# The sum of a bank's two halves one step behind ScalarE's copy, and modulation sums at most one per half tile

## The chip, the cores and the metric

The kernel runs on one core of a Trainium2 chip. A core has TensorE (PE, matrix products into PSUM), VectorE (DVE), ScalarE (ACT), GpSimd (POOL) and SyncE (SP, which issues most DMAs). Each engine works through its own queue in order and waits for the others by semaphores. The metric is the device time of one execution in microseconds (us); less is better.

## The reference

One decoder layer on 256 tokens of width 2048, in float32. A vector `c` gives six modulation rows; the part that this study is about is the token mixer.

```python
mod = silu(c) @ w_ada + b_ada            # 6 rows of 2048: shift, scale, gate, twice
h = rms_norm(x, norm1_g) * (1 + scale1) + shift1
proj = h @ w_in                          # (256, 2048) @ (2048, 9248)
lru_x = causal_conv(proj[lru x columns])
lru_out = gelu(proj[lru gate columns]) * rg_lru(lru_x, ...)
ssd_out = mamba2_heads(proj[z], proj[x, B, C], proj[dt], ...)
x = x + gate1 * (concat(lru_out, ssd_out) @ w_out)
h2 = rms_norm(x, norm2_g) * (1 + scale2) + shift2
x = x + gate2 * peer(h2, ...)            # top-16 experts of 16384 for 8 heads
out = rms_norm(x, final_norm_g)
```

In `mamba2_heads` the z columns go through `silu`; in the LRU part the gate columns go through `gelu`. These two kinds of columns are those whose evacuation is changed.

## The kernel before

**Exact products from rounded operands.** Weights come from memory in pieces of 128x1024 (`raw`). ScalarE copies a piece to a rounded high half `hl[:, 0]` (line 144), VectorE subtracts it from the raw piece and gets the low half `hl[:, 1]` (line 153, called "low half" below). The activations `hT` (tile `H`) are kept as a high and a low half too. A product is the sum of high x high, high x low and low x high. There are four buffers for `raw` and four for `hl`. In each half tile `issue_split` issues the high half of the piece four half tiles ahead, which has to wait until TensorE has left its buffer, then the low half of the piece before that one, three half tiles ahead; behind the low half the DMA of a new `raw` goes into SP's queue.

**Tiles.** The input projection makes 73 column tiles of 128 columns by 256 tokens, in the order of `ETILES`: first the SSD tiles with the SSD steps of four groups between them, then the LRU tiles. The first twelve go through `w_pass`, the other 61 (slots 0 to 60) through a loop of two half tiles each (`for h in range(2)`, lines 782 to 810), in PSUM bank `slot % 3`. Tiles of x, B, C, and LRU x are 256 columns wide in PSUM and take three matmuls per block (lines 796 to 798). Tiles of z (`32 <= e < 48`) and of the LRU gate (`e < 16`) take two, one of 512 columns that has high x high in the left half and high x low in the right half of the bank, and one of 256 (lines 449 and 451, `wide`). For those, the two halves of the bank have to be added. Of these 512-wide tiles the loop makes 26: 13 of z and 13 of the LRU gate.

**Order of the side work.** The program is written in the order in which each engine takes it. `defer(f, d)` puts `f` into a list that is run d half tiles after the next call of `mid()`; `mid()` runs once per half tile, behind `issue_split`. At the end of each tile its evacuation (`evac`) is deferred, so it runs in the first half of the next tile. What an evacuation defers in its turn runs in the second half. `bg_pop` takes one step of the SSD and LRU work per tile: its TensorE part at once, the rest deferred. The names that matter below:

- `halves(o, ps)`, lines 453 to 455: ScalarE copies the bank's right half to `o`, VectorE adds the left half to it; `o` is `ggt` (LRU gate) or the z tile (`X`, `zs`).
- `silu2`, lines 431 to 439: tanh on ScalarE into `stmp`, the product on VectorE one step later.
- `conv`, lines 421 to 429: ScalarE's first tap, three taps on VectorE one step later (line 426).
- `ada_step`, lines 378 to 407: one modulation step, a 128x1024 multiply-add on VectorE (line 389; line 386 for the first of sixteen), and the DMA of a new `adr` piece (two buffers). After sixteen, `fin` has 8 small matmuls (line 398) into the bank of the tile before (into bank 6 from slot 44).
- `ada_tick(rate, slot)`, lines 410 to 414: adds the rate (0.65 per SSD tile, 1.1 per LRU tile, 0.74 in the output projection) to a credit and runs a step for each whole credit.
- `lru_gates`: the matmuls of line 651, which read the conv's result `xct`; `lru_scan`: line 671 to 685; SSD: `Dm` (line 569), then the matmuls of lines 577 to 579.

Of the kernel before, what the change touches and what calls it, by code (L numbers as in the profile page):

```python
# [14 lines left out]
AF = mybir.ActivationFunctionType  # L15
OP = mybir.AluOpType
# [14 lines left out]
ADA_SSD, ADA_LRU, ADA_OUT = 0.65, 1.1, 0.74  # L31
# [27 lines left out]
def hybrid_kernel(ctx, tc, xT, cols, w_ada, w_in, lru_w, w_o1, w_o2, w_q, keys, u_t, v_t, fng, out):  # L59
    nc = tc.nc  # L60
    pe, act, dve, pool, sp = nc.tensor, nc.scalar, nc.vector, nc.gpsimd, nc.sync
# [9 lines left out]
    def bank(n):  # L71
        return psum.tile([128, 512], FT, name=f"b{n}")
# [3 lines left out]
    def xbuf(i):  # L76
        return pair[:, 4 * i:4 * i + 4] if i < 2 else keep.tile([128, 4, 256], FT, name=f"X{i}")
# [8 lines left out]
    def col(name, i=0, n=1):  # L86
        o, w = COLS[name]
        return cc[:, o + i:o + i + n]
# [78 lines left out]
    def defer(f, d=0):  # L167
        stages[d].append(f)
# [209 lines left out]
    def ada_step(slot):  # L378
        u = ada["use"]
        if u >= len(adq):  # L380
            return
        s, h, k = adq[u]
        w = adr.pop(u)
        if k == 0:
            ada["acc"] = mix.tile([128, 1024], FT, name="adacc", bufs=2)
            dve.tensor_scalar(ada["acc"], w, cact[:, 0:1], None, op0=OP.mult)
        else:
            a = ada["acc"]
            dve.scalar_tensor_tensor(a, w, cact[:, k:k + 1], a, op0=OP.mult, op1=OP.add)  # L389
        ada["use"] += 1  # L390
        ada_dma()
        if k == 15:
            a = ada["acc"]

            def fin():
                p = bank(ada["bank"])
                for i in range(8):
                    pe.matmul(p[:, i:i + 1], a[:, i * 128:(i + 1) * 128], ones[:, 0:1], start=True, stop=True)

                def add():  # L400
                    m = mod[:, s, 8 * h:8 * h + 8]
                    dve.tensor_add(m, p[:, :8], col("b_ada", 16 * s + 8 * h, 8))
                    if s == 3:
                        dve.scalar_tensor_tensor(m, m, 1.0, col("g2", 8 * h, 8), op0=OP.add, op1=OP.mult)
                defer(add)
            pedue.append((slot + 2, fin))

    adt = [0.0]

    def ada_tick(rate, slot):  # L410
        adt[0] += rate
        while adt[0] >= 1.0:
            adt[0] -= 1.0
            ada_step(slot)

# [5 lines left out]
    def conv(o, ps, w, bcol, after=None):  # L421
        act.activation(o, ps, AF.Identity, scale=w[3], bias=bcol)

        def taps():
            for d in (1, 2, 3):
                dve.scalar_tensor_tensor(o[:, d:], ps[:, :T - d], w[3 - d], o[:, d:], op0=OP.mult, op1=OP.add)
            if after:
                defer(after)
        defer(taps)

    def silu2(o, u, x, scale, on_pool):
        S["nt"] = (S["nt"] + 1) % 2
        t = S["tmp"][:, 2 + S["nt"]]
        act.activation(t, u, AF.Tanh, scale=scale)

        def pool_fin():
            pool.tensor_tensor(t, t, x, op=OP.mult)
            pool.tensor_tensor(o, t, x, op=OP.add)
        defer(pool_fin if on_pool else lambda: dve.scalar_tensor_tensor(o, t, 1.0, x, op0=OP.add, op1=OP.mult))
# [13 lines left out]
    def halves(o, ps):  # L453
        act.activation(o, ps[:, 256:], AF.Copy)
        dve.tensor_tensor(o, ps[:, :256], o, op=OP.add)

    S = {}
    acd = ctx.enter_context(tc.tile_pool(name="acd", bufs=1, space=bass.MemoryType.DRAM)).tile(
# [181 lines left out]
    LR = {"w": {}, "gg": {}}  # L640

    def lru_gates(b, i):
        h = 4 * b + i
        xc = LR["xc"][:, i]
        Z = {}

        def g_pe():
            w = LR["w"].pop(h)
            Z["p"] = p = bank(4 - (i + GD) % 2)
            for s in range(2):  # L650
                pe.matmul(p[:, s * 256:(s + 1) * 256], w[:, s], xc, start=True, stop=True)
            lru_w_load()

        def g_ew():
            if i == 0:
                LR.update(a=xbuf(0),
                          m=xbuf(1),
                          gx=keep.tile([128, 4, 256], FT, name="X2"))
            r, gx, p = LR["a"][:, i], LR["gx"][:, i], Z["p"]
            act.activation(r, p[:, :256], AF.Sigmoid, bias=col("lba", h))  # L660
            act.activation(gx, p[:, 256:], AF.Sigmoid, bias=col("lbi", h))
            act.activation(LR["m"][:, i], r, AF.Tanh, scale=lsp[:, h:h + 1])
            pool.tensor_tensor(gx, gx, xc, op=OP.mult)
        return g_pe, g_ew, 0
# [54 lines left out]
    def evac(e, ps):  # L719
        nonlocal y_ssd  # L720
        if e == 72:
            y_ssd = mix.tile([128, 16, 2, 256], FR, name="yssd", tag="Y1")
            S["BCs"] = mix.tile([128, 2, 2, 256], FT, name="BCs", tag=L[6])
            S["tmp"] = mix.tile([128, 4, 256], FT, name="stmp", tag=L[7])
            S["nt"] = 0
            dt_evac(ps)
        elif e >= 48:
            after = None
            if e >= 64:
                g = e % 4  # L730
                if e < 68:
                    S["BC"] = S["BCs"][:, g % 2]
                    for n, t in enumerate(("xs", "zs")):
                        S[t] = (mix.tile([128, 4, 256], FT, name=t) if g == 3 else
                                xbuf(2 * (g % 2) + n))
                o = S["BC"][:, (e - 64) // 4]
            else:
                i = e % 4
                g = (e - 48) // 4
                o = S["xs"][:, i]  # L740
                if i == 3:
                    ssd_steps(g)
            conv(o, ps, [hcw[:, (e - 48) * 4 + i:(e - 48) * 4 + i + 1] for i in range(4)],
                 hcb[:, e - 48:e - 47], lambda: silu2(o, o, o, 1.0, g == 0 or e < 64))
        elif e >= 32:
            i = e % 4
            o = S["zs"][:, i]
            if ps.shape[1] == 512:
                halves(o, ps)
                defer(lambda: silu2(o, o, o, 0.5, False))  # L750
            else:
                silu2(o, ps, ps, 0.5, False)
        elif e >= 16:
            b, i = divmod(e - 16, 4)
            if i == 0:
                LR["xc"] = mix.tile([128, 4, 256], FT, name="xct", tag="aa", bufs=3)
            conv(LR["xc"][:, i], ps, [col("lcw", (e - 16) * 4 + i_) for i_ in range(4)], col("lcb", e - 16))
            bg2.extend([(None, None, 0)] * (GD * (e == 16)) + [lru_gates(b, i)])
            if i == 3:
                bg2.extend(lru_scan(b) + lru_out(b))  # L760
        else:
            b, i = divmod(e, 4)
            if i == 0:
                LR["gg"][b] = mix.tile([128, 4, 256], FT, name="ggt", tag=(L[3], L[7], L[6], "aa")[b],
                                    bufs=3 if b == 3 else 1)
            if ps.shape[1] == 512:
                halves(LR["gg"][b][:, i], ps)
            else:
                act.activation(LR["gg"][b][:, i], ps, AF.Copy)

# [10 lines left out]
    slot = 0  # L781
    for e in ETILES[N0:]:
        ps = bank(slot % 3)
        two = e < 16 or 32 <= e < 48
        if not two:
            ps = ps[:, :256]
        for h in range(2):
            w = take()
            for kk in range(8):
                k = 8 * h + kk  # L790
                wh = w[:, 0, kk * 128:(kk + 1) * 128]
                wl = w[:, 1, kk * 128:(kk + 1) * 128]
                if two:
                    wide(ps, w, kk, hT, k)
                    continue
                pe.matmul(ps, wh, hT[:, k, 0, :], start=(k == 0), stop=False)  # L796
                pe.matmul(ps, wh, hT[:, k, 1, :], start=False, stop=False)  # L797
                pe.matmul(ps, wl, hT[:, k, 0, :], start=False, stop=(k == 15))  # L798
            issue_split()
            mid()  # L800
            if h == 0 and slot > 0:
                ada_tick(ADA_SSD if e >= 32 else ADA_LRU, slot)
        if e == 62:
            for _ in range(2):
                lru_w_load()
        bg_pop()
        ada["bank"] = 6 if slot >= 44 else (slot + 2) % 3
        pe_due(slot)
        defer(lambda e=e, ps=ps: evac(e, ps))
        slot += 1  # L810
# [54 lines left out]
    for n, k in enumerate(korder):  # L865
        w = take()
        y = y_ssd[:, k - 16] if k >= 16 else y_lru[k // 2][:, k % 2]
        for d in range(8):
            o = ob[d // 2][:, (d % 2) * 256:(d % 2) * 256 + 256]
# [38 lines left out]
    for d in range(8, 16):  # L908
        ps = bank(3 + d % 2)
# [735 lines left out]
```

## Time and profile before

| | us |
|---|---|
| median of 3 runs | 2152.05 |
| lowest and highest | 2142.25, 2161.91 |
| the profiled execution | 2157.51 |
| its span, first to last instruction | 2155.8 |
| idle of TensorE from 160 to 560 us | 14.3 |
| busy time of VectorE there | 328.8 of 400 |

The profile is one execution. A row names the line, engine and operation, the tiles written and read ("out<-in"), and for idle time the engine that ended it. [...] Where an instruction waits for several engines, the profile names the one that came last by its own reckoning, which need not be the right one. The stretch from 160 to 560 us holds the loop over the tiles. Its granted clock is given as a share of TensorE's full clock.

### The profile page before, as it was taken

The page shows a single profiled execution, that of the slowest core. Times are in us where ns is not written, and L with a number is a line of the kernel's source. Part 1 is how long each engine was busy: PE and PEld are TensorE (multiplying, and loading weights), DVE is VectorE, ACT ScalarE, POOL GpSimd, SP SyncE. Part 2 cuts the span into 40 slices and gives each one's busy share as a digit, 9 for nine tenths or more (in the row PEclk, how much of TensorE's full clock was granted, in tenths as well). Part 3 has the DMA queues.
Part 4 walks back from the last instruction along what each step waited for, and adds up shares of the span by engine and source line. Part 5 has one row for each costly group of instructions (what it writes and reads, how often), then busy time and mean ns, then how long its engine had stood idle before and what let it go on. Part 6 is the DMA issues. An engine that isn't in the chain of part 4 may idle for free.

```text
span 2155.8 us, 34802 instructions
## 1 busy us (share of the span) xinstructions
PE 2085.5 (97%) x13060; PEld 1633.2 (76%) x13060; DVE 1397.8 (65%) x2009; ACT 964.9 (45%) x1472; POOL 887.8 (41%) x728
## 2 busy tenths in 40 slices
PE   7999999999999999999999999999999999999996
PEld 4789989988999898888788778666666656555653
DVE  3378887977888869779889986433334353343434
ACT  3356656666644454444445444333333333333332
POOL 0013133412112110002325641777777757777774
PEclk9999999999999999999999999999999999999998
DMA  9967666767789955677777778899999999999996
GB/s 388 406 224 247 211 218 224 257 223 247 265 306 344 323 181 176 202 242 254 253 259 234 237 266 282 302 360 339 334 348 348 345 329 344 359 371 345 347 342 232
DMA packets 250615, 620.54 MB, mean 288 GB/s; under 512 B 38024, under 2 KB 122168, under 8 KB 228152
## 3 DMA queue, kind: packets, MB, share of 16 engines
q1 hardware_dynamic: 188992, 387.76, 52.0%
q0 software_dynamic: 45056, 175.52, 22.3%
q10 hardware_dynamic: 16400, 55.06, 7.7%
q8 instruction: 102, 1.67, 0.3%
q14 instruction: 65, 0.53, 0.1%
HBM read 696.60 MB, written 14.72 MB: 330 GB/s over the span
## 4 chain that ended last, share of the span: by engine, by line
PE 70%; DMA 9%; DVE 9%; issue 5%; ACT 3%; POOL 2%; another core or an unknown queue 1%; SPq 0%; POOLq 0%; DVEq 0%; ACTq 0%
PE b L449 14%; PE b L1397 9%; PE b L1483 7%; PE b L451 7%; PE b L1323 4%; PE b L1325 4%; PE b L1324 4%; DVE hl L153 4%; PE b L918 3%; DMA raw<-in_w_in 2%; PE b L796 2%; PE b L797 2%; PE b L798 2%; PE b L919 1%; DMA adw<-in_w_ada 1%
## 5 line engine op out<-in xcount | busy, mean ns | idle before, releaser
L144 ACT ACTIVATE hl<-raw 128x1024 fp32r<-128x1024 f32 x594 | 628.0, 1059 | 1058.4 <-PE b L451 198.2
L153 DVE TENSOR_TENSOR hl<-raw,hl 128x1024 fp32r<-128x1024 f32 x594 | 764.7, 1297 | 133.9 <-ACT hl L144 119.5
L449 PE MATMUL b<-H,hl 128*128 128x512 f32 x1376 | 495.1, 403 | 0.1
L451 PE MATMUL b<-H,hl 128*128 128x256 f32 x1376 | 386.8, 281 | 3.9 <-DVE hl L153 3.6
L1376 POOL DMA_INDIRECT X<-ad,X x256 | 297.2, 1161 | 87.7 <-issue 74.4
L449 PEld LDWEIGHTS b<-H,hl 128*128 128x128 f32 x1376 | 259.6, 189 | 87.1 <-issue 19.2
L1483 PE MATMUL b<-hl,X 128*128 128x512 f32 x1152 | 276.9, 397 | 12.3 <-ACT X L442 9.7
L1483 PEld LDWEIGHTS b<-hl,X 128*128 128x128 f32 x1152 | 213.7, 189 | 88.3 <-issue 27.3
L451 PEld LDWEIGHTS b<-H,hl 128*128 128x128 f32 x1376 | 261.0, 190 | 6.5 <-DVE hl L153 5.0
L1323 PE MATMUL b<-hl,H 128*128 128x512 f32 x640 | 253.3, 396 | 0.0
L1325 PE MATMUL b<-hl,H 128*128 128x512 f32 x640 | 250.3, 391 | 2.5 <-DVE hl L153 2.5
L1324 PE MATMUL b<-hl,H 128*128 128x512 f32 x640 | 250.2, 391 | 0.0
L1367 POOL DMA_INDIRECT vq<-in_v_t,X x128 | 150.0, 1172 | 112.8 <-DVE vq L1537 39.0
L1367 POOL DMA_INDIRECT tk<-in_v_t,X x128 | 144.8, 1132 | 70.9 <-issue 32.3
L798 PE MATMUL b<-H,hl 128*128 128x256 f32 x560 | 160.2, 286 | 4.4 <-DVE hl L153 4.4
L796 PE MATMUL b<-H,hl 128*128 128x256 f32 x560 | 163.3, 292 | 0.0
L797 PE MATMUL b<-H,hl 128*128 128x256 f32 x560 | 159.9, 286 | 0.0
L1387 DVE TENSOR_TENSOR Wz<-X 128x4 f32<-128x4 f32 x64 | 10.8, 169 | 224.7 <-DMA X<-ad,X 98.6
L1325 PEld LDWEIGHTS b<-hl,H 128*128 128x128 f32 x640 | 120.6, 188 | 29.2 <-DVE hl L153 4.0
L389 DVE SCALAR_TENSOR_TENSOR adacc<-adr,cact,adacc 128x1024 f32<-128x1024 f32 x90 | 127.6, 1418 | 19.3 <-DMA adr<-in_w_ada 19.0
L1323 PEld LDWEIGHTS b<-hl,H 128*128 128x128 f32 x640 | 120.6, 188 | 23.9
L1324 PEld LDWEIGHTS b<-hl,H 128*128 128x128 f32 x640 | 120.6, 188 | 23.9
(324 smaller groups left out, 3163.2 us busy)
## 6 DMA issues: line engine op xcount, KB each, us to landing
raw<-in_u_t SPq DMA_DIRECT2D x208, 512.0 KB
raw<-in_w_in SPq DMA_DIRECT2D x146, 512.0 KB
adr<-in_w_ada SPq DMA_DIRECT2D x96, 512.0 KB
adw<-in_w_ada SPq DMA_DIRECT2D x64, 512.0 KB
raw<-in_w_o SPq DMA_DIRECT2D x64, 512.0 KB
raw<-in_u_t ACTq DMA_DIRECT2D x48, 512.0 KB
raw<-in_v_t SPq DMA_DIRECT2D x48, 512.0 KB
raw<-in_v_t ACTq DMA_DIRECT2D x48, 512.0 KB
```

The source lines that it names most:

```text
L144: act.activation(t[:, 0], r, AF.Copy)
L153: dve.tensor_sub(t[:, 1], r, t[:, 0].bitcast(FT))
L449: pe.matmul(ps, w[:, 0, c], x[:, k].rearrange("p a b -> p (a b)"), start=(k == first), stop=False, skip_group_check=True)
L451: pe.matmul(ps[:, :256], w[:, 1, c], x[:, k, 0], start=False, stop=(k == 15), skip_group_check=True)
L796: pe.matmul(ps, wh, hT[:, k, 0, :], start=(k == 0), stop=False)
L798: pe.matmul(ps, wl, hT[:, k, 0, :], start=False, stop=(k == 15))
L1323: pe.matmul(o, hh, w[:, 0, :, kk], start=(k == 0), stop=False)
L1324: pe.matmul(o, hl_, w[:, 0, :, kk], start=False, stop=False)
L1325: pe.matmul(o, hh, w[:, 1, :, kk], start=False, stop=(k == 15))
L1367: pool.indirect_dma_start(x, None, vf, bass.IndirectOffsetOnAxis(ap=eV[:, t:t + 1], axis=0), bounds_check=E1 - 1, oob_is_err=False)
L1376: pool.indirect_dma_start(wA[:, n:n + 1], None, adf, bass.IndirectOffsetOnAxis(ap=eW[:, t:t + 1], axis=0), bounds_check=T * E1 - 1, oob_is ...
L1483: pe.matmul(ob[tb * 2 + c], w[:, i, s], v[:, k, c * 512:(c + 1) * 512], start=(jj == 0 and (i, k) == (0, 0)), stop=(jj == JD - 1 and k == 1))
```

## The change

Two edits. First, in the loop's z and LRU gate tiles the sum of the two halves no longer follows the copy at once: `halves_apart` issues the copy on ScalarE and defers the add by one half tile. For a z tile the tanh is deferred behind the add, so it comes one half tile later as well, and the product behind the tanh too. The other callers of `halves` (the query tiles and the dense expert tiles later on) are not touched. Second, `ada_tick` runs at most one step at a call, and is called in both halves of a tile, in the second with a rate of 0: a second whole credit is spent there.

```diff
     def ada_tick(rate, slot):
         adt[0] += rate
-        while adt[0] >= 1.0:
+        if adt[0] >= 1.0:
             adt[0] -= 1.0
             ada_step(slot)
...
+    def halves_apart(o, ps, then=None):
+        act.activation(o, ps[:, 256:], AF.Copy)
+
+        def add():
+            dve.tensor_tensor(o, ps[:, :256], o, op=OP.add)
+            if then:
+                defer(then)
+        defer(add)
...
             if ps.shape[1] == 512:
-                halves(o, ps)
-                defer(lambda: silu2(o, o, o, 0.5, False))
+                halves_apart(o, ps, lambda: silu2(o, o, o, 0.5, False))
...
             if ps.shape[1] == 512:
-                halves(LR["gg"][b][:, i], ps)
+                halves_apart(LR["gg"][b][:, i], ps)
...
-            if h == 0 and slot > 0:
-                ada_tick(ADA_SSD if e >= 32 else ADA_LRU, slot)
+            if slot > 0:
+                ada_tick(0.0 if h else ADA_SSD if e >= 32 else ADA_LRU, slot)
```

Behind the new function the line numbers of the changed kernel are 9 higher up to line 755 of the old, and 8 higher from there; the add is line 461 there. What each engine gets is the same set of instructions in another order.

First place: VectorE's queue around the first `lru_scan` (line 675, 684 in the changed kernel), before. `ggt` are LRU gate tiles, `adacc` is a modulation step, `rstd` belongs to the last SSD group.

```order
L455 TENSOR_TENSOR ggt<-b_4303,ggt 128x256
L389 SCALAR_TENSOR_TENSOR adacc<-adr,cact,adacc 128x1024
L153 TENSOR_TENSOR hl<-raw,hl 128x1024 x2
L455 TENSOR_TENSOR ggt<-b_4369,ggt 128x256
L389 SCALAR_TENSOR_TENSOR adacc<-adr,cact,adacc 128x1024
L153 TENSOR_TENSOR hl<-raw,hl 128x1024
L602 RECIPROCAL rstd<-rstd 128x256
L675 SCALAR_TENSOR_TENSOR X_72<-X_4449,X_72 128x1024
L153 TENSOR_TENSOR hl<-raw,hl 128x1024
```

The same place in the changed kernel, from the step that now stands ahead of the first of these adds:

```order
L389 SCALAR_TENSOR_TENSOR adacc<-adr,cact,adacc 128x1024
L153 TENSOR_TENSOR hl<-raw,hl 128x1024
L461 TENSOR_TENSOR ggt<-b_4303,ggt 128x256
L153 TENSOR_TENSOR hl<-raw,hl 128x1024
L389 SCALAR_TENSOR_TENSOR adacc<-adr,cact,adacc 128x1024
L153 TENSOR_TENSOR hl<-raw,hl 128x1024
L611 RECIPROCAL rstd<-rstd 128x256
L684 SCALAR_TENSOR_TENSOR X_72<-X_4449,X_72 128x1024
L461 TENSOR_TENSOR ggt<-b_4369,ggt 128x256
L153 TENSOR_TENSOR hl<-raw,hl 128x1024
```

The add of the second tile (`b_4369`) stood ahead of a modulation step, a low half, the reciprocal and line 675; now it stands behind all four.

Second place: VectorE's queue around the second `lru_scan`, before, with the conv of an LRU x tile (`xct`) behind it.

```order
L455 TENSOR_TENSOR ggt<-b_4808,ggt 128x256
L389 SCALAR_TENSOR_TENSOR adacc<-adr,cact,adacc 128x1024
L153 TENSOR_TENSOR hl<-raw,hl 128x1024
L675 SCALAR_TENSOR_TENSOR X_72<-X_4890,X_72 128x1024
L153 TENSOR_TENSOR hl<-raw,hl 128x1024
L389 SCALAR_TENSOR_TENSOR adacc<-adr,cact,adacc 128x1024 x2
L153 TENSOR_TENSOR hl<-raw,hl 128x1024
L426 SCALAR_TENSOR_TENSOR xct<-b_4860,cc,xct 128x255
```

The same place in the changed kernel:

```order
L389 SCALAR_TENSOR_TENSOR adacc<-adr,cact,adacc 128x1024
L153 TENSOR_TENSOR hl<-raw,hl 128x1024
L684 SCALAR_TENSOR_TENSOR X_72<-X_4890,X_72 128x1024
L461 TENSOR_TENSOR ggt<-b_4808,ggt 128x256
L153 TENSOR_TENSOR hl<-raw,hl 128x1024
L389 SCALAR_TENSOR_TENSOR adacc<-adr,cact,adacc 128x1024
L153 TENSOR_TENSOR hl<-raw,hl 128x1024
L426 SCALAR_TENSOR_TENSOR xct<-b_4860,cc,xct 128x255
L426 SCALAR_TENSOR_TENSOR xct<-b_4860,cc,xct 128x254
L426 SCALAR_TENSOR_TENSOR xct<-b_4860,cc,xct 128x253
L389 SCALAR_TENSOR_TENSOR adacc<-adr,cact,adacc 128x1024
```

The add stands behind line 675, and the second of the two modulation steps stands behind the taps (line 426). Such a pair of steps is parted at three places of the program.

## The prediction

> **What bounds the kernel now.** I read the page first, then the busy time by stage, then who waits for whom in the stage that the change touches, and last the timelines around its stalls.
>
> ```profile
> span 2155.8 us, 34802 instructions
> PE 2085.5 (97%) x13060; PEld 1633.2 (76%) x13060; DVE 1397.8 (65%) x2009; ACT 964.9 (45%) x1472; POOL 887.8 (41%) x728
> ```
>
> TensorE is busy for 97% of the span, so only time in which it stands still, or runs at a lowered clock, can be won by moving work of other engines. The change touches the SSD and LRU part of the input projection, which runs from about 160 to 560 us. The next rows are windows of that part and of the places in it where TensorE stood: start and end, length, busy time (with the number of instructions) of TensorE, its weight loads, VectorE, ScalarE and GpSimd, then TensorE's granted clock, the DMA share and GB/s.
>
> ```profile
> 160.00:560.00 400.00, 385.67 (x2733) 355.96 (x2731) 328.76 (x405) 254.89 (x424) 115.84 (x90) 0.98 0.71 232
> 265.00:275.00 10.00, 8.05 (x53) 7.16 (x53) 9.38 (x13) 6.84 (x15) 4.17 (x4) 0.83 0.68 198
> 320.00:340.00 20.00, 17.95 (x133) 16.62 (x132) 14.46 (x22) 10.77 (x24) 5.36 (x6) 0.91 0.73 252
> 390.00:395.00 5.00, 4.29 (x40) 4.12 (x40) 4.93 (x7) 4.05 (x10) 0.96 (x1) 1.00 0.96 318
> 440.00:475.00 35.00, 30.64 (x179) 26.61 (x178) 32.46 (x37) 23.37 (x33) 7.43 (x4) 0.95 0.58 191
> 500.00:510.00 10.00, 6.49 (x30) 5.96 (x29) 9.93 (x13) 4.35 (x5) 2.70 (x2) 0.66 0.71 224
> 550.00:560.00 10.00, 8.24 (x65) 7.86 (x64) 9.93 (x13) 6.24 (x9) 3.86 (x1) 1.00 0.78 262
> ```
>
> The reader is to see that 400 us hold only 400 - 385.67 = 14.3 us of standing, all of it in the six short windows (1.95 + 2.05 + 0.71 + 4.36 + 3.51 + 1.76). Four of them also have a lowered clock, which costs about length x (1 - clock): 1.7, 1.8, 1.75 and 3.4 us, together 8.65. So 14.3 + 8.65 = 23 us is all that this part can give, 1.07% of 2152.05. Whatever shares of other engines look like, no reordering here is worth more.
>
> Who is waited for, in the same 400 us, TensorE's rows first, then VectorE's (engine, line, releaser: total us, times, longest):
>
> ```profile
> PE b L651 <- ACT xct L422: 3.5, 1, 3.5
> PE b L798 <- DVE hl L153: 3.1, 3, 1.5
> PE b L451 <- DVE hl L153: 1.2, 1, 1.2
> ...
> PE b L579 <- ACT xdest L550: 1.0, 1, 1.0
> ...
> PE b L651 <- DMA wai<-in_lru_w: 0.8, 1, 0.8
> PE b L398 <- DVE zs L455: 0.7, 1, 0.7
> ...
> DVE ggt L455 <- ACT ggt L454: 24.9, 10, 6.8
> DVE X L455 <- ACT X L454: 22.0, 7, 4.8
> DVE zs L455 <- ACT zs L454: 8.1, 3, 3.4
> ```
>
> VectorE stands 24.9 + 22.0 + 8.1 = 55 us in front of the add of line 455, waiting for ScalarE's copy of the other half bank. That is not TensorE's time: the weights (hl) are split four half tiles ahead. It matters only where VectorE's backlog eats those four.
>
> **The wait that the change removes.** Two adds of gate tiles show it. Timeline rows (start, us, engine, line, operation; in brackets idle before it), VectorE, then ScalarE, then TensorE:
>
> ```profile
> 432.48 2.36 DVE L153 TENSOR_TENSOR hl<-raw,hl 128x1024 fp32r<-128x1024 f32 x2
> 441.68 0.42 DVE L455 TENSOR_TENSOR ggt<-b,ggt 128x256 f32<-128x256 f32 x1 [6.84 <-ACT ggt L454]
> 442.02 1.28 DVE L389 SCALAR_TENSOR_TENSOR adacc<-adr,cact,adacc 128x1024 f32<-128x1024 f32 x1
> 443.21 1.22 DVE L153 TENSOR_TENSOR hl<-raw,hl 128x1024 fp32r<-128x1024 f32 x1
> 444.35 1.75 DVE L602 RECIPROCAL rstd<-rstd 128x256 f32<-128x256 f32 x1
> 446.01 1.17 DVE L675 SCALAR_TENSOR_TENSOR X<-X,X 128x1024 f32<-128x1024 f32 x1
> ...
> 434.43 1.06 ACT L144 ACTIVATE hl<-raw 128x1024 fp32r<-128x1024 f32 x1 [2.15 <-PE b L451]
> 441.28 0.36 ACT L454 ACTIVATE ggt<-b 128x256 f32<-128x256 f32 x1
> ...
> 444.49 0.38 PE L798 MATMUL b<-H,hl 128*128 128x256 f32 x1 [1.54 <-DVE hl L153]
> ```
>
> The low half at 443.21 needs the high half that ScalarE wrote from 434.43 to 435.49. It could have run nearly eight microseconds sooner; it stands behind the add, and the add behind a ScalarE queue of table loads and exponentials. TensorE then waits 1.54 us for it. In the changed order (the first place shown above) the modulation step (1.28), this low half (1.22) and the reciprocal (1.75) stand ahead of the add and fit into the 6.84 us of idling: 4.25 us of VectorE's work is done while it stood still. From there on VectorE hardly idles (32.46 of the 35 us from 440 to 475 are busy, and the first 1.7 of the rest lie ahead of 441.68), so what follows moves up with it, and the next low halves too.
>
> The second place, rows of the same kind:
>
> ```profile
> 491.81 0.42 DVE L455 TENSOR_TENSOR ggt<-b,ggt 128x256 f32<-128x256 f32 x1 [4.67 <-ACT ggt L454]
> 496.75 4.63 DVE L389 SCALAR_TENSOR_TENSOR adacc<-adr,cact,adacc 128x1024 f32<-128x1024 f32 x2
> 502.44 1.50 DVE L426 SCALAR_TENSOR_TENSOR xct<-b,cc,xct 128x255 f32<-128x255 f32 x3
> ...
> 486.34 1.06 ACT L144 ACTIVATE hl<-raw 128x1024 fp32r<-128x1024 f32 x1 [1.97 <-DMA raw<-in_w_in]
> 496.70 0.55 ACT L422 ACTIVATE xct<-b,cc 128x256 f32<-128x256 f32 x1
> ...
> 504.05 2.05 PE L651 MATMUL b<-xct,wai 128*128 128x256 f32 x4 [3.51 <-ACT xct L422]
> ```
>
> The profile puts TensorE's 3.51 us down to ScalarE's L422, but the L422 of this tile ended at 497.25. What ends just before 504.05 is the three conv taps, at 502.44 + 1.50 = 503.94, and the gates read their result. The taps waited for two modulation steps in one half tile, 4.63 us. In the changed order one of the two stands behind the taps (half of 4.63, 2.3 us), and a step and a low half (1.28 + 1.22) go into the 4.67 us of idling: the taps move up by 2.3 + 2.5 = 4.8 us, more than the 3.51. They can't start before 497.25, which leaves room.
>
> The third kind, an SSD tile (VectorE, then TensorE):
>
> ```profile
> 265.55 0.42 DVE L455 TENSOR_TENSOR X<-b,X 128x256 f32<-128x256 f32 x1 [4.76 <-ACT X L454]
> 267.08 2.35 DVE L153 TENSOR_TENSOR hl<-raw,hl 128x1024 fp32r<-128x1024 f32 x2
> 269.69 0.69 DVE L569 TENSOR_TENSOR Dm<-Dm,cbt 128x512 f32<-128x512 f32 x1
> ...
> 270.52 0.44 PE L577 MATMUL b<-Dm,xdt 128*64 128x128 f32 x2 [1.95 <-ACT X L422]
> ...
> 368.95 0.42 DVE L455 TENSOR_TENSOR zs<-b,zs 128x256 f32<-128x256 f32 x1 [3.37 <-ACT zs L454]
> 541.11 0.42 DVE L455 TENSOR_TENSOR ggt<-b,ggt 128x256 f32<-128x256 f32 x1 [4.65 <-ACT ggt L454]
> ```
>
> Here L577 needs Dm, made from 269.69 to 270.38. A modulation step, a low half (2.5 us of the 4.76 idle) and the tanh product that now comes later (0.4, an add's size) leave its path: about 2 us sooner is all of the 1.95. The last two rows are the same idling ahead of the stalls at 390 to 395 and at 550 to 560 us.
>
> **The sum.** Idle removed: 1.95 (265) + 0.71 (390) + 4.36 - 0.8 (440; the 0.8 for the LRU weights' DMA stays) + 3.51 (500) + 1.76 (550) = 11.5 us. The window at 320 keeps its 2.05: it waits for ScalarE's own work and for the copy itself. Clock: 1.7 at 265 and 3.4 at 500 return with their stalls, 5.1 us; the 1.8 and 1.75 of the other two I leave. Together 16.6 us.
>
> Against that stands what the moved add makes late. Nothing is added or removed: 26 copies, 26 adds and every modulation step with its DMA remain; SP's queue only gets three modulation loads one weight load later, each with a second buffer for cover. But each add is now behind a low half and, in places, behind a reciprocal and a line 675, and the bank that it empties is written again by the first matmul two tiles on, the very half tile for which that low half is due. ScalarE's tanh of a z tile waits for the add as well and has a weight copy (1.06) queued behind it; it goes one half tile later along with the add, so that wait is not lengthened. The modulation sums' matmuls (L398) take the bank of the tile before, too: L398 already waits 0.7 for such an add. Bounds for the whole: none at all, if the adds are covered everywhere, up to 26 x 0.42 = 10.9 us. I take 0.66 (the 0.7 of L398, the one row of a wait on such an add) at seven places, about as many as the stalls that go (one each at 265, 390 and 500, two each at 440 and 550): 4.6 us. So 16.6 - 4.6 = 12.0 us.
>
> [...]
>
> The profiled execution took 2157.5 us with its span of 2155.8, 5.5 above the median of the three runs (2152.05). The 12.0 us come off either; TensorE is the bound after 560 us, so they stay off. Forecast: 2152.05 - 12 = 2140 us.
>
> **The rivals.** (a) The wait only moves. VectorE's work is the same, and where TensorE waits most VectorE is near its limit; once its head start is used, the next stall takes the place of the old, as ScalarE's queue (copies waiting for a raw weight: 1.97 us at 486.34) decides. For it: 32.46 of 35 us busy from 440 on, and 9.93 of 10 from 500 and from 550. Against it: 55 us of standing is there to be used. It keeps 3 of 16.6 us: 2149 us.
>
> (b) Slower: the add becomes the last thing before a PSUM bank's reuse. If in each of the 26 tiles VectorE comes to the add later than TensorE to the bank, each costs its 0.42, 10.9 us, and the stalls of today remain: 2152 + 11 = 2163 us. It decides from the point at which VectorE runs a whole lead (three half tiles) late; the rows show that only at the seven stalls, so it is unlikely.
>
> (c) Everything goes, with the clock windows at 320 and 440 too: 23 us, 2129 us. Against it: 1.0 us at 320 (L579) is ScalarE's and 0.8 a DMA's.
>
> **How the numbers follow.** Forecast 0.62, (a) 0.22, (b) 0.08, (c) 0.08. The three runs before lie from 2142.25 to 2161.91, about 10 us either way, which goes on top of each case. The range 2130 to 2155 holds the forecast and (a) with most of that spread and leaves out (b) and most of (c). About 1% (21.5 us) is what a measurement of this kernel can tell from no change. Faster by more than that, below 2130.5, is (c) and the forecast's lower edge: 0.12. Slower by more, above 2173.6, needs (b) and a bad spread: 0.02. The rest, 0.86, is within 1%.
>
> **What would show it.** Right: VectorE's wait for ScalarE's copy falls from 55 us to under 15; no 1.54 us wait of L798 near 444, no 3.5 us wait of L651 near 504; TensorE's standing from 160 to 560 us falls from 14.3 to 5 to 8 us, and the clock at 500 to 510 is 1.00. Wrong: first matmuls of a tile (L449, L796) wait for the moved add, or new waits of L651 or L577 on ScalarE of the size of those that went. The forecast is wrong as well if this part gets shorter and the kernel doesn't, which would mean that the later stages are bound by their DMA and not by TensorE.

## The result and the profile after

| | before | changed |
|---|---|---|
| median of 15 runs each, us | 2154.03 | 2139.87 |
| lowest to highest | 2142.25 to 2161.91 | 2133.11 to 2149.13 |
| the profiled execution | 2157.51 | 2143.90 |
| loop over the tiles, first to last start of its first matmul | 423.9 | 408.5 |

The ratio is 0.9936, with an interval of 0.9920 to 0.9952: 0.64% faster, 13.8 us of 2154. The forecast was 12 us off and 2140.0; that the changed median lies within 0.2 us of it is luck, since the median before has moved by 2.0 us as well. In the experiments below, four executions of the kernel before took 3096 to 7184 us and are left out of its medians and of the ratios.

The page of the changed kernel, then its window of 160 to 560 us (start and end, length, busy time of TensorE, weight loads, VectorE, ScalarE and GpSimd, clock, DMA share, GB/s):

```profile
span 2142.2 us, 34793 instructions
PE 2083.1 (97%) x13060; PEld 1633.4 (76%) x13060; DVE 1399.7 (65%) x2009; ACT 963.6 (45%) x1472; POOL 891.8 (42%) x728
```

```profile
160.00:560.00 400.00, 394.33 (x2855) 365.85 (x2854) 347.17 (x425) 263.77 (x438) 133.86 (x93) 1.00 0.72 243
```

The numbers of instructions of the five engines are the old ones, and each engine's busy time is within 4 us of the old. TensorE stood 5.7 of the 400 us instead of 14.3, and did more in them (2855 matmul records instead of 2733). VectorE is busy for 347.2 instead of 328.8 us of this stretch: the same work, closer together, and since the loop ends earlier, nearly 8 us at the end of the stretch now belong to the output projection.

Who waits for whom in the tile loop of the changed kernel, TensorE's rows and, of VectorE's, those of the moved add:

```profile
PE b L398 <- DVE zs L461: 1.9, 1, 1.9
PE b L586 <- DVE Dm L578: 1.3, 1, 1.3
PE b L449 <- ACT X L670: 1.1, 1, 1.1
PE b L660 <- ACT X L669: 0.7, 1, 0.7
PE b L804 <- DVE ggt L461: 0.4, 1, 0.4
...
DVE zs L461 <- ACT zs L458: 2.3, 1, 2.3
DVE X L461 <- ACT X L458: 1.4, 2, 0.9
DVE ggt L461 <- ACT ggt L458: 0.2, 1, 0.2
```

The 55 us that the add waited for ScalarE's copy are 3.9. The two long stalls of before, of 3.5 and 1.5 us, are not in the list, nor is any wait for a low half. In their place stand a wait of L398 that is nearly three times the old one, and a first matmul (L804) that waits for the add itself. VectorE's idling did not go with the add's wait: it still stands 52.8 of the 400 us instead of 71.2, and now most of all in front of the low half itself, while ScalarE makes the high half (18.3 us, 3.6 before). There it costs nothing, since no matmul of the list waits for a low half.

The place around the first `lru_scan`, timeline of VectorE and one row of TensorE (start, us; in brackets idle before; "x3" is three like instructions in a row; spans of one engine overlap, as line 684 ends at 440.68, 0.08 us behind the start of the add):

```profile
433.55 1.23 DVE L153 TENSOR_TENSOR hl<-raw,hl 128x1024 fp32r<-128x1024 f32 x1 [0.26 <-ACT hl L144]
435.34 1.75 DVE L611 RECIPROCAL rstd<-rstd 128x256 f32<-128x256 f32 x1 [0.56 <-ACT rstd L610]
439.45 1.23 DVE L684 SCALAR_TENSOR_TENSOR X<-X,X 128x1024 f32<-128x1024 f32 x1 [2.36 <-ACT X L681]
440.60 0.42 DVE L461 TENSOR_TENSOR ggt<-b,ggt 128x256 f32<-128x256 f32 x1
...
441.16 0.35 PE L804 MATMUL b<-H,hl 128*128 128x256 f32 x1 [0.42 <-DVE ggt L461]
```

The low half that ended at 444.4 before now ends at 434.8 (the first row); 2.0 us of that are the whole program's lead at this point (ScalarE's copy for it begins at 432.45 instead of 434.43), the rest is its place in the queue. What TensorE meets here instead is the bank: the add ends at 441.02 and the first matmul of the tile that writes the same bank starts at 441.16, 0.42 us late. 1.54 + 0.74 us of stalls for low halves became 0.42 for the add.

The place around the second `lru_scan`, where the two modulation steps stood together, rows of the same kind:

```profile
484.32 1.23 DVE L684 SCALAR_TENSOR_TENSOR X<-X,X 128x1024 f32<-128x1024 f32 x1 [2.88 <-ACT X L681]
485.46 0.42 DVE L461 TENSOR_TENSOR ggt<-b,ggt 128x256 f32<-128x256 f32 x1
485.79 1.22 DVE L153 TENSOR_TENSOR hl<-raw,hl 128x1024 fp32r<-128x1024 f32 x1
486.93 1.28 DVE L389 SCALAR_TENSOR_TENSOR adacc<-adr,cact,adacc 128x1024 f32<-128x1024 f32 x1
488.12 1.22 DVE L153 TENSOR_TENSOR hl<-raw,hl 128x1024 fp32r<-128x1024 f32 x1
489.31 1.52 DVE L426 SCALAR_TENSOR_TENSOR xct<-b,cc,xct 128x255 f32<-128x255 f32 x3
490.75 1.94 DVE L389 SCALAR_TENSOR_TENSOR adacc<-adr,cact,adacc 128x1024 f32<-128x1024 f32 x1
...
493.32 1.02 PE L660 MATMUL b<-xct,wai 128*128 128x256 f32 x4
```

From the add to the end of the taps it is 485.46 to 490.83, 5.4 us; before it was 491.81 to 503.94, 12.1. The gates (L660) begin 2.5 us behind the taps with no idle time in brackets, where TensorE had stood 3.51 us.

The length of the loop, from the line view of the first of its three matmuls, before and after (count, duration in ns, first and last start):

```profile
L796 PE MATMUL b<-H,hl x560: 278/283/775, 141.9 to 565.8; 128*128 128x256 f32 x187
```

```profile
L804 PE MATMUL b<-H,hl x560: 280/283/681, 142.9 to 551.4; 128*128 128x256 f32 x187
```

Where did the rest of the execution go? The loop is 15.4 us shorter, the output projection behind it took 199.0 us instead of 194.5 (first L880 at 552.4 to first L960 at 751.4; before, lines 872 and 952, 566.8 and 761.3), and the part from the first matmul of the last loop (line 1483 before, 1491 now; at 1729.1 and 1721.8) to the end took 420.4 instead of 426.7. Second profiles (below) have 192.9 for the output projection in both kernels, and 414.7 before and 417.1 changed for the last part. So neither that loss nor that gain belongs to the change; single executions differ by 6 and 12 us in these two parts.

### The profile page after: what moved, and what is told of

Its sections match the earlier page's. It is cut to its first block, busy times and chain, and to the rows that moved or that the text cites. A ratio compares the mean times of both kernels' runs of the same rounds, so it can differ in the third digit from the quotient of the medians.

```text
span 2142.2 us, 34793 instructions
## 1 busy us (share of the span) xinstructions
PE 2083.1 (97%) x13060; PEld 1633.4 (76%) x13060; DVE 1399.7 (65%) x2009; ACT 963.6 (45%) x1472; POOL 891.8 (42%) x728
## 4 chain that ended last, share of the span: by engine, by line
PE 72%; DVE 10%; DMA 9%; issue 4%; ACT 3%; POOL 2%; SPq 0%; another core or an unknown queue 0%; POOLq 0%; DVEq 0%; ACTq 0%
PE b L449 14%; PE b L1491 11%; PE b L1405 10%; PE b L451 7%; DVE hl L153 4%; PE b L1331 4%; PE b L1333 4%; PE b L1332 4%; PE b L804 2%; PE b L806 2%; PE b L805 2%; PE b L926 2%; DMA adr<-in_w_ada 2%; DMA two<-in_w_ada 2%; DMA raw<-in_w_in 1%
## 5 line engine op out<-in xcount | busy, mean ns | idle before, releaser
L449 PE MATMUL b<-H,hl 128*128 128x512 f32 x1376 | 492.9, 402 | 1.3 <-ACT X L670 1.1
L449 PEld LDWEIGHTS b<-H,hl 128*128 128x128 f32 x1376 | 258.4, 188 | 88.4 <-issue 18.1
L804 PE MATMUL b<-H,hl 128*128 128x256 f32 x560 | 162.4, 290 | 0.4 <-DVE ggt L461 0.4
```

The source lines that it names most:

```text
L449: pe.matmul(ps, w[:, 0, c], x[:, k].rearrange("p a b -> p (a b)"), start=(k == first), stop=False, skip_group_check=True)
```

## Experiments

All times beside the kernel before on the same chip. The first four experiments below share one set of runs of it (median 2134.89 us), the next four another (2135.08), the last three, the kernel before among them, a third (2134.13); these runs are faster than those above on either kernel, so ratios are compared across groups, not times. "Idle" is TensorE's standing time from 160 to 550 us, "low clock" the sum of length x (1 - clock) over windows of 5 us there, "loop" the time from the first to the last start of the first of the loop's three matmuls (line 796 before) in the one profile.

| kernel | ratio and interval | loop | idle | low clock |
|---|---|---|---|---|
| before (profile of the prediction) | 1 | 423.9 | 12.6 | 8.5 |
| before, second profile | 1.0007 (0.9987 to 1.0026) | 425.3 | 14.7 | 5.2 |
| whole change | 0.9936 (0.9920 to 0.9952) | 408.5 | 5.7 | 1.7 |
| whole change, second | 0.9925 (0.9906 to 0.9944) | 407.9 | 4.0 | 3.5 |
| deferred add alone | 0.9919 (0.9904 to 0.9933) | 408.8 | 7.5 | 0 |
| deferred add alone, second | 0.9932 (0.9915 to 0.9950) | 412.5 | 9.6 | 1.7 |
| parted steps alone | 0.9997 (0.9982 to 1.0012) | 418.6 | 13.3 | 1.7 |
| add deferred in gate tiles alone | 0.9937 (0.9923 to 0.9950) | 412.6 | 7.8 | 3.4 |
| add deferred in z tiles alone | 0.9987 (0.9973 to 1.0002) | 419.8 | 11.1 | 5.1 |
| whole change, L398 in bank 3 | 0.9911 (0.9891 to 0.9931) | 405.2 | 4.2 | 0 |
| add alone, L398 in bank 3 | 0.9928 (0.9909 to 0.9946) | 409.2 | 6.3 | 1.7 |
| bank 3, add two half tiles behind | 0.9941 (0.9922 to 0.9960) | 411.9 | 7.9 | 3.4 |
| bank 3, add three half tiles behind | 0.9980 (0.9965 to 0.9994) | 421.1 | 15.3 | 3.4 |

**The deferred add alone.** The tick is put back:

```diff
-        if adt[0] >= 1.0:
+        while adt[0] >= 1.0:
...
-            if slot > 0:
-                ada_tick(0.0 if h else ADA_SSD if e >= 32 else ADA_LRU, slot)
+            if h == 0 and slot > 0:
+                ada_tick(ADA_SSD if e >= 32 else ADA_LRU, slot)
```

> The deferred add alone; the modulation credit is spent as before, two steps in one half tile where two are due. Theory (the gain is low halves and taps that no longer stand behind an add waiting for ScalarE): about 12 us faster than before, nearly all of the 13.8 us of the whole change. The stall of 3.5 us near 504 shrinks to about 1 us, since 2.5 us of the 4.8 us that the taps had to move up come from the add. Rival (the gain is the parted modulation steps, since the largest stall and the longest low clock stood behind such a pair): 7 us or less, and a stall of 3 us or more is left in the second LRU group.

0.9919: the gain is there, in this group as large as that of the whole change above. Of the 3.51 us in front of the gates' matmuls (L651 before, L660 here) 0.93 is left, as the theory had it (the profile names ScalarE, but the taps that the matmuls read end at 491.92, 0.11 us ahead of them):

```profile
492.03 1.10 PE L660 MATMUL b<-xct,wai 128*128 128x256 f32 x4 [0.93 <-ACT ggt L702]
```

**The parted modulation steps alone** (the tick of the change, `halves` everywhere).

> The parted modulation steps alone; copy and add stay together. Theory: only the stall near 504 can shorten, by the 2.3 us of one modulation step, and some of its 3.4 us of low clock: 2 to 5 us faster than before, and VectorE still waits about 55 us for ScalarE's copies. Rival (the parted steps carry the gain): 7 us or more. A third way: nothing, because the second step only delays the next low half: within 1 us.

0.9997: nothing that can be measured, the third way by its time, but not by its mechanism. The taps behind the parted step (first two rows) came in time, and the stall of 3.51 us at their gates is gone. In its place the gates of the next tile wait 2.28 us for their own taps:

```profile
495.68 1.52 DVE L426 SCALAR_TENSOR_TENSOR xct<-b,cc,xct 128x255 f32<-128x255 f32 x3
497.30 1.10 PE L651 MATMUL b<-xct,wai 128*128 128x256 f32 x4
...
504.82 1.50 DVE L426 SCALAR_TENSOR_TENSOR xct<-b,cc,xct 128x255 f32<-128x255 f32 x3
506.42 1.10 PE L651 MATMUL b<-xct,wai 128*128 128x256 f32 x4 [2.28 <-issue]
```

Here the wait moved on by one tile, and TensorE still stood 13.3 us in all. The 1.2 us by which 2.28 is less than 3.51 are below what the interval, 3.2 us either way, can show.

**The add deferred in one kind of tile**, with the old tick; in the first the z tiles, in the second the gate tiles use `halves` again:

```diff
-                halves_apart(o, ps, lambda: silu2(o, o, o, 0.5, False))
+                halves(o, ps)
+                defer(lambda: silu2(o, o, o, 0.5, False))
```

```diff
-                halves_apart(LR["gg"][b][:, i], ps)
+                halves(LR["gg"][b][:, i], ps)
```

> The add deferred in the 13 LRU gate tiles alone, z tiles and modulation steps as before. Theory: the stalls near 444 to 463 (3.5 us), the larger part of the one near 504 (with its clock 5 us) and those near 550 (1.8 us) go: 8 us faster than before, two thirds of the whole. Rival (each of the 26 adds carries an equal part of the gain, whatever stall lies behind it): 6 us here and 6 us with the z tiles alone.

> The add deferred in the 13 z tiles alone, LRU gate tiles and modulation steps as before. Theory: only the stalls near 270 (1.95 us and 1.7 us of low clock) and 394 (0.7 us) go: 4 us faster than before, less what L398's wait near 332 costs more (1.2 us). Rival (equal parts): 6 us.

Gate tiles: 0.9937, 13.5 us, more than the expected 8. Z tiles: 0.9987, 2.8 us, and the interval holds zero. So the adds don't carry equal parts, and the theory had the order right but gave the gate tiles too little. The 22.0 + 8.1 us that VectorE waited in front of the z tiles' adds were mostly worth nothing, the 24.9 us in front of the gate tiles' adds nearly everything: the places around `lru_scan` are those where ScalarE's queue holds the add (6.84 and 4.67 us before) and TensorE then waits, 1.54 us at the first, where the split weights' lead is used up, and 3.51 us at the second, for the taps (read from the timelines; no run changes ScalarE's queue alone). Who waits with the gate tiles alone changed (VectorE's rows of both adds):

```profile
DVE X L455 <- ACT X L454: 18.6, 7, 4.4
DVE zs L455 <- ACT zs L454: 8.6, 3, 3.4
DVE ggt L461 <- ACT ggt L458: 0.2, 1, 0.2
```

There VectorE still stands 27 us in front of the z tiles' adds, and by the intervals the kernel can't be told from the whole change.

**The whole change and the add alone, side by side.**

> The whole change once more, to stand beside the deferred add alone on one chip and to give a second profile of it. If the parted modulation steps are worth nothing (parted alone they gave a ratio of 0.9997): as fast as the deferred add alone, within 3 us. If they cost something once the adds are deferred (the first ratios were 0.9936 for the whole change and 0.9919 for the add alone): 3 to 4 us slower than it. The output projection, which took 199.0 us in the profile of the whole change and 194.5 before: near 194.5 if that was one execution's low clock, near 199 if the change costs it.

> The deferred add alone once more, on the same chip as the whole change. As above: equal to the whole change within 3 us, or 3 to 4 us faster. Its profile shows how far idle time and low clock between 160 and 560 us differ between two executions of the same program: about 8.5 us idle again, since waits are set by the order of the queues, and another low clock than the first time (none) if that depends on where an idle gap happens to fall.

The medians are 2117.40 and 2119.95 us, 2.6 us apart in favour of the whole change; with L398 in bank 3 (next) 2115.14 and 2119.45, 4.3 us apart. The intervals of the ratios overlap in both pairs, but all four kernels ran in one group, so their runs can be compared without the kernel before: over both pairs the means are 3.1 us apart, with an interval of 1.4 to 4.8 (resampling the six runs of each). The profiles point the same way: the whole change idles 4.0 to 5.7 us, the add alone 7.5 to 9.6. So the parted steps, worth nothing alone, probably add some 3 us behind deferred adds; the cost that the first ratios seemed to show, from two different groups, is not there.

**The small matmuls in bank 3.** L398 of the first modulation row goes to a bank that no tile uses:

```diff
-        ada["bank"] = 6 if slot >= 44 else (slot + 2) % 3
+        ada["bank"] = 6 if slot >= 44 else 3 if slot < 33 else (slot + 2) % 3
```

> The whole change, and the first modulation row's small matmuls (L398) go to bank 3, which is unused up to that point, instead of the bank of the tile before, so that they don't wait for the moved add. If that wait is the price of the deferral (1.9 us, and up to 1.7 us of low clock behind it): 2 to 3.5 us faster than the whole change, and no wait of L398 near 332. If ScalarE's copy, which was itself late, would hold TensorE at another place: within 1 us.

> The deferred add alone with the small matmuls in bank 3. If the parted steps are worth nothing and the bank is worth something, this is the fastest of the four, by 1 to 3 us. If the parted steps help once the adds are deferred, the whole change with bank 3 is faster than this one by 2 us or more.

With the whole change: 2.3 us faster in the median (2115.14 against 2117.40) and the lowest ratio of all, 0.9911, though the intervals overlap. L398 is gone from TensorE's waits, and the loop is the shortest, 405.2 us. With the add alone: 0.5 us, nothing.

The expectation took L398's wait for the price of the deferral. The traces say otherwise. The copy in front of that add stands in ScalarE's queue behind line 561 (570 in the changed kernel), which waits for the DMA of `rb`, issued by ScalarE itself. Before, then in the whole change:

```profile
330.38 1.28 ACT L561 ACTIVATE Dm<-rb,scols 128x128 f32<-128x128 f32 x4 [0.23 <-DMA rb<-acd]
333.36 1.92 PE L398 MATMUL b<-ones,adacc 128*128 128x1 f32 x16 [0.66 <-DVE zs L455]
```

```profile
329.15 1.28 ACT L570 ACTIVATE Dm<-rb,scols 128x128 f32<-128x128 f32 x4 [1.43 <-DMA rb<-acd]
332.13 1.92 PE L398 MATMUL b<-ones,adacc 128*128 128x1 f32 x16 [1.86 <-DVE zs L461]
```

L398 waits 0.43 us longer than line 561 or 570 does in both, and to 0.01 us in all seven profiles in which L398 uses a tile's bank and that DMA is late (0.23 to 1.43 us); where it is not late, with the parted steps alone and with the z tiles alone, L398 waits 0.38 and 0.41. With the add deferred alone its wait was 0.68 and 1.03 in two profiles. So its size follows this DMA and not the deferral.

**The kernel before, once more.**

> The kernel before, once more, for a second profile of it. Idle time of TensorE from 160 to 550 us is set by the order of the queues: 12 to 13 us again, with the same stalls. The clock: if a lowered clock belongs to the stall behind which it stands, about 8.5 us of it again; if it depends on where a gap falls, another figure, as in the profiles of the changed kernels (0 to 3.5 us for the same two programs).

Idle time 14.7 instead of 12.6 us and low clock 5.2 instead of 8.5. The stalls are not quite the same ones either: that at 462 was 2.63 instead of 1.15 us, one of 1.89 at 415 is new, and that at 265 was 1.36 instead of 1.95. So the order of the queues alone does not fix the waits of one execution. For the clock, the row to look at is the window around the stall at 265, here and in the kernel with the parted steps alone, which has the same queue at this place (columns as above); the prediction showed 8.05 us busy at a clock of 0.83 for it:

```profile
265.00:275.00 10.00, 8.64 (x64) 7.69 (x62) 9.93 (x13) 7.16 (x16) 4.07 (x3) 1.00 0.75 254
```

```profile
265.00:275.00 10.00, 7.81 (x59) 6.95 (x58) 9.82 (x13) 7.16 (x15) 4.17 (x4) 1.00 0.74 235
```

In the second a stall of 2.19 us kept the full clock where one of 1.95 had lost it.

**The add later still**, two and three half tiles behind the copy, with L398 in bank 3 (it would otherwise write the bank ahead of the add). In the first:

```diff
-        defer(add)
+        defer(add, 1)
```

and `defer(add, 2)` in the second.

> The changed kernel with L398 in bank 3, and the add of the z and gate tiles one further half tile later (two behind the copy). If the add is covered with a half tile to spare: within 2 us of the kernel with bank 3 alone (ratio 0.991 to before). If the bank's reuse already decides (the price of the slower rival): first matmuls of a tile wait for the add, and half or more of the gain is gone (ratio 0.995 or more).

> The same with the add three half tiles behind the copy, the last place before the bank is written again. The low half ahead of it on VectorE can only be made some 2.3 us into the half tile before the reuse, and the add ends 2.7 us into its 2.8. So, if the mechanism of the slower rival is right, nearly every one of the 26 tiles makes its successor wait, by 0.4 to 1.5 us: 10 to 40 us slower than with bank 3 alone, slower than before or level with it. If the add is covered there too: within 3 us of bank 3.

Two behind: 0.9941, between the two ratios expected, with 0.30% less gain than bank 3 alone, though the intervals (0.9891 to 0.9931 and 0.9922 to 0.9960) just overlap and the runs are of two groups. Three behind: 0.9980, nearly all lost. One place shows how. VectorE's add of the gate tile at the first `lru_scan`, and the first matmul that writes its bank, two behind, then three behind (one behind was shown above: 440.60 and 441.16, idle 0.42; with L398 in bank 3 it is 436.14 and 436.70, idle 0.42 as well):

```profile
438.69 0.42 DVE L461 TENSOR_TENSOR ggt<-b,ggt 128x256 f32<-128x256 f32 x1
...
439.26 0.40 PE L804 MATMUL b<-H,hl 128*128 128x256 f32 x1 [3.22 <-ACT X L687]
```

```profile
446.21 0.42 DVE L461 TENSOR_TENSOR ggt<-b,ggt 128x256 f32<-128x256 f32 x1
...
446.77 0.55 PE L804 MATMUL b<-H,hl 128*128 128x256 f32 x1 [4.62 <-ACT yssd L620]
```

Each time the matmul starts 0.14 to 0.15 us behind the add's end, whatever engine the profile names, and TensorE's wait grows from 0.42 over 3.22 to 4.62 us, as more of VectorE's queue (four products of line 626, a modulation step, a low half) comes to stand ahead of the add. The expectation for three behind, that nearly every one of 26 tiles waits, was wrong: in TensorE's waits of that kernel there are nine places, 13.8 us in all, if the three put down to ScalarE's line 620 are counted as the one above was read; those are enough.

```profile
PE b L804 <- ACT yssd L620: 7.3, 3, 4.6
PE b L804 <- DVE ggt L461: 5.1, 4, 1.7
...
PE b L449 <- DVE X L461: 0.7, 1, 0.7
PE b L449 <- DVE zs L461: 0.7, 1, 0.7
```

## Why the prediction was right

**The bound** (23 us at most) held: the loop got 15.4 us shorter in one pair of profiles and 17.4 in the other (425.3 to 407.9).

**The add's wait and the low half behind it.** Right, and shown by taking the parts apart: the deferred add alone gives 0.9919 and 0.9932 where the whole change gives 0.9936 and 0.9925, and the gate tiles alone give nearly all of that. The place at 441 went as worked out. Of the 4.36 us of standing from 440 to 475, of which 0.8 were to stay, 1.5 are left: 0.42 for the bank and 1.07 of a new wait of L449, at 463.79. The profile puts that down to ScalarE's line 670, which ends at 463.80, too late to be it; three taps of line 426 end at 463.64, 0.15 us ahead of the matmul. This looks like one more wait for a bank, but no run tests it. The 0.8 us for the LRU weights' DMA did not stay.

**The taps at the gates.** The mechanism was right: with both parts the matmuls L660 start at 493.3 without a wait. Measured against the moment at which TensorE was ready for them, the taps ended 3.4 us late before and 2.5 us early now, 5.9 us sooner where 4.8 were forecast. The add's share is 2.6 us (3.51 to 0.93), where 2.5 were forecast. The parted step alone took the whole 3.51 away at this place, where 2.3 were forecast: the pair of 4.63 us that the prediction halved was one step of 1.28 us and one of 3.31. It was worth nothing alone because the next tile's gates then waited 2.28 us, which is the rival (a), the wait that only moves, at one place. With the add alone the two next gates of the group wait 0.37 and 0.66 us; with both parts only the last waits, 0.67.

**The SSD tile at 265.** The 1.95 us went, but its successor is now late (L586, 1.3 us, in the list of waits above): the z tiles' idling bought 2.8 us, not the 1.95 + 0.71 + 1.7 = 4.4 of the sum, with an interval that holds both and zero. The term left out is a DMA. In front of that late step line 570 waited 2.48 us for `rb`; in the second profile of the whole change it waited 0.32 at the same place, and L586 did not wait. ScalarE's waits for this DMA in the 400 us come to 3.3 and 8.2 us in the two profiles of the kernel before, and to 8.2 to 16.6 us in those of the whole change and of the add alone. So in the SSD tiles this transfer is probably the next limit; no run changes it.

**The sum of idle time.** 11.5 removed less 4.6 made, 6.9 us net, were forecast. TensorE's idle from 160 to 560 us fell from 14.3 to 5.7, 8.6 us. That forecast and gain lie within 2 us of each other is in part luck: the price was about 4 us too large (next), while waits came that the sum does not have, of 1.3 (L586), 1.07 (L449), 0.67 (L660) and 0.3 us (L606), and L398's grew by 1.2.

**The price of lateness.** 4.6 us, as seven waits of 0.66. This is the term that was wrong. One wait on a moved add came that the deferral made, 0.42 us (L804); the other wait on such an add, L398's, from which the 0.66 were taken, follows the DMA of `rb` as shown above, so that its growth to 1.9 us is no price of lateness either. The last experiments show that the rival's mechanism, the reuse of the bank, is real (L804 waited 3.22 and 4.62 us, to 0.14 or 0.15 us behind the add's end); at the first `lru_scan` the change already touches it, with that 0.42.

**The clock.** 5.1 us were forecast, as what comes back with two particular stalls. As a sum this is near what was seen (8.5 to 1.7 in one pair, 5.2 to 3.5 in the other, 4.3 us in the mean), but that is luck, for only one of the two stalls behaved as assumed. At the gates the working held: the three profiles with a stall of 3.51 to 3.65 us there (the kernel before twice, the z tiles alone) lose 3.4, 1.7 and 1.7 us behind it, and no other profile loses any there. At 265 it did not: the first profile lost 1.7 us, the second, with a stall of 1.36, nothing, and the parted steps alone nothing with one of 2.19.

The length of a stall does not settle it either. All five stalls of 3.2 to 4.6 us in the loops of the thirteen profiles lost clock, but one of 3.10, at 416 in the second profile of the add alone, lost none; of the eight from 1.9 to 2.8 us (L398 aside) five did. That the loss depends on where a gap falls, as the expectations of the second profiles allow, would fit them, but no run tests it. By these counts a clock term can be forecast as a mean over stalls of a length, and not for one stall of 2 us.

**The parted steps** were counted within the taps alone. They are worth nothing without the deferred add, and probably some 3 us with it; the size stays open.

**What a measurement can tell.** The prediction took about 1% for it. The interval is 0.16% either way, so the gain of 0.64% is clear of noise.

## What to carry to other kernels

An instruction that waits for another engine's slow queue should not stand ahead of work that the bound engine needs: issue its partner first and itself one step later, when its input is already there. It pays only where the wait uses up the lead of what stands behind it; here 25 us of idling in one kind of tile were worth nearly all and 30 us in another almost nothing. The step has an end, the point at which what it reads is written again: with L398 out of the way one half tile later won 0.9%, two 0.6% (their intervals just overlap), three 0.2%, and a buffer that somebody else writes sooner (the bank of L398) is to be looked for first. And before a wait is called the price of a change, follow it back through the queue of the engine that it is put down to: L398's began at a DMA.

## What the hardware showed that was not expected

TensorE's granted clock differs between executions at the same stall: 0.83 over the window at 265 to 275 us in one profile of the kernel before (a stall of 1.95 us), 1.00 in another (1.36), and 1.00 with a longer stall (2.19) in a kernel with the same queue there. A low stretch, where it comes, is one of about 3.4 us at half the clock and costs 1.7 us, or two of them: in the changed kernel the clock is 0.50 from 334.5 to 337.5 us and 1.00 again from 338. Between two executions the low clock in the loop differed by 1.7 to 3.3 us, as much as the parts of this change that could not be settled.

In eight of the thirteen profiles such a stretch begins within the 16 matmuls of L398 or right behind them, at about 330 us; each of them is 128x1, and together they take 2 to 3 us. In two of the eight (the z tiles alone, the add alone with bank 3) TensorE had waited 0.41 us or not at all in front of them, so a stall alone is not what the stretch follows there. Why the other five have none stays open.
